# Sixteen transposes of a token pair in one burst; four PSUM banks for transposes and four for accumulators

## The chip, the cores and the metric

The kernel runs on one core of a Trainium2 chip. The metric is the time of one execution on the device in microseconds (us); of several runs the median is given. Beside the plain runs there is one profiled execution, from which the trace comes.

## The reference

One layer over 4096 prompt rows and 32 sample rows of width 1024, in float32:

```
h = RMSNorm(x) * norm_g
u, v, z_a, xb, z_b = split(h @ w_in)              # w_in is 1024 x 5120, five parts of 1024
v_n = LayerNorm(v)
a = u * (W_spatial v_n + b_spatial) * silu(z_a)   # per head and per chunk of 128 rows, masked
b = scale * group_linear(trailing_mean(xb) - xb) * silu(z_b)   # windows 2, 4, 8, 16
x = x + concat(a, b) @ w_out
y = RMSNorm(x) * final_g
```

Outputs are y for both groups of rows, the last rows of xb, and the normalised v rows of the sample group. The change lies where h and v are made for the prompt rows.

## The kernel before, in words

All large products are made by a scheme of seven products of 2 x 2 blocks (instead of eight), and each float32 operand is split into a high part that is rounded to the format of TensorE's fast pass (a cast on ScalarE, L479 for the rows, L119 for weights) and a low part, the rest (a subtraction on VectorE, L81). One product of the seven, numbered q = 0 to 6, is four steps along the contraction times three terms (high by high, high by low, low by high): twelve matmuls of 128 x 128 by 512 columns on L193.

The first stage (L211 to L613) takes about the first 398 us. It opens with the preparation of weights: the rows of w_in for xb times the pooling weights ("comb", transposes on L402 and products on L261), the rows of the past (L384), and the seven weight operands `wv` of v. Then it goes through sixteen pairs of row blocks, blocks 1, 2, 3, 0 of 1024 rows and four pairs in each. A pair is two tiles of 128 rows, 512 rows apart, called z = 0 and 1. For each pair:

- `load` brings the two tiles `xt` from DRAM on SP's queue (L466). There are four buffers for them, so two pairs' worth.
- `norms` takes the sum of squares on ScalarE (L294), the inverse root on VectorE (L86 to L91) and scales `xt` in place on VectorE (L307). The same call finishes LayerNorm of the v of an earlier pair: statistics on VectorE (L300, L301, L310), scaling on ScalarE (L312), and then two stores to `v_all` that ScalarE's queue issues (L538).
- `quarter(z, kh)` turns half a tile: four transposes of 128 x 128 on TensorE (L473) into one PSUM bank `tr`.
- `operands` returns seven steps. They make the seven left operands from the four quarters: x11, x12 and x22 directly from the bank, x21 by a copy on ScalarE (L502), and four sums on VectorE (L507, L508, L509, L516). Each operand is then split into an `op` tile and stored for later stages on SP's queue (L485, or L488 for the last block).
- `product(q)` runs the twelve matmuls into an accumulator bank `acc`, and `Combine.after(q)` puts the result together in the two tiles `vt` of v. For q 0, 2 and 4 ScalarE copies the bank (L167, L172, L174), otherwise VectorE adds it (L165, called from L169 on). Products 0, 2 and 4 share one bank, 3 and 6 another, 1 and 5 have one each: four banks for a pair. Product 6 adds on top of what product 3 left, after VectorE has read that.

While the products of pair n run, the steps of pair n + 1 are issued, one ahead of each product. So in the program's text each product has at most one quarter ahead of it. The first pair's operands are made in the opening. The last two pairs run interleaved (`lagged`), since there is no later pair to prepare: eight accumulators are then asked for, from the same pool. The text's order is not the order on the engines: a scheduler of the framework sets that, and also which buffer of a pool a tile gets, by its own costs. A tile that asks a full pool for a buffer waits for the last reader of the one it is given.

PSUM has eight banks of 128 x 512 float32. In the first stage three are in `ps_tr` (tag "tr") and five in `ps_acc` (tag "acc").

Of the kernel before, what the change touches and what calls it, by code (L numbers as in the profile page):

```python
# [36 lines left out]
def stream_step(ctx: ExitStack, tc, x_prompt, x_sample, state_pool, norm_g, w_in, ln_v_g, ln_v_b,  # L37
# [167 lines left out]
    def pool(name, bufs, stack=ctx, **kw):  # L205
        return stack.enter_context(tc.tile_pool(name=name, bufs=bufs, reuse_waits="tile", **kw))
# [4 lines left out]
    with ExitStack() as ph:  # L211
# [2 lines left out]
        e_p = ph.enter_context(tc.tile_pool(name="e_p", bufs=1))  # L214
        h_p = ph.enter_context(tc.tile_pool(name="h_p", bufs=6))
        op_p = ph.enter_context(tc.tile_pool(name="op_p", bufs=9))
        ps_tr = ph.enter_context(tc.tile_pool(name="ps_tr", bufs=3, space=bass.MemoryType.PSUM))
        ps_acc = ph.enter_context(tc.tile_pool(name="ps_acc", bufs=5, space=bass.MemoryType.PSUM))

        def xtile(dt=F32):  # L220
            return xt_p.tile([P, D], dt, tag="xt", name="xt")
# [1 line left out]
        def vtile():  # L223
            return v_p.tile([P, D], F32, tag="vt", name="vt")
# [4 lines left out]
        def half(dt=F32):  # L229
            return h_p.tile([P, HALF], dt, tag="h", name="h")  # L230
# [4 lines left out]
        def tr_tile():  # L235
            return ps_tr.tile([P, 512], F32, tag="tr", name="tr")
# [7 lines left out]
        def load_rows(i):  # L244
            rows_t[i] = vtile()
            nc.sync.dma_start(rows_t[i], w_in[0, i * P:(i + 1) * P, 3 * D:4 * D])
# [21 lines left out]
        def load_v_weights(c):  # L268
            v_raws[c] = a, b = [t.rearrange("p (k e) -> p k e", e=P)
                                for t in (op(F32), op(F32))]  # L270
            c0 = D + c * P
            nc.sync.dma_start(a, w_in_v[:, :, c0:c0 + P])
            nc.sync.dma_start(b, w_in_v[:, :, c0 + 512:c0 + 512 + P])
# [113 lines left out]
        pairs = []  # L387
# [69 lines left out]
        class Pair:  # L457
# [11 lines left out]
            def quarter(self, z, kh):  # L469
                tr = tr_tile()  # L470
                for kk in range(4):
                    k = 4 * kh + kk
                    nc.tensor.transpose(tr[:, kk * P:(kk + 1) * P], self.x[z][:, k * P:(k + 1) * P], ident)  # L473
                return tr
# [12 lines left out]
                    dst = xops_l[q, :, :, self.j * P:(self.j + 1) * P]  # L487
                    nc.sync.dma_start(dst, t.rearrange("p h (k t) -> p (h k) t", t=P).bitcast(F32))  # L488

            def operands(self):  # L490

                self.ops, k = {}, {}
                tt = nc.vector.tensor_tensor

                def one():
                    k["x11"] = self.quarter(0, 0)
                    self.split(0, k["x11"])

                def two():
                    x21 = self.quarter(1, 0)  # L500
                    k["x21"] = half()
                    nc.scalar.copy(k["x21"], x21)  # L502

                def three():
                    k["x22"] = self.quarter(1, 1)
                    k["s1"], k["s2"] = half(), half()
                    tt(k["s1"], k["x22"], k["x21"], ALU.add)  # L507
                    tt(k["s2"], k["s1"], k["x11"], ALU.subtract)  # L508
                    tt(k["x21"], k["x11"], k["x21"], ALU.subtract)  # L509

                    self.split(2, k["s2"])

                def four():
                    x12 = self.quarter(0, 1)
                    self.split(1, x12)
                    tt(k["s2"], x12, k["s2"], ALU.subtract)  # L516

                def five():
                    self.split(6, k["x22"])
                    self.split(3, k["x21"])  # L520

                return [one, two, three, four, five, lambda: self.split(4, k["s1"]), lambda: self.split(5, k["s2"])]

            def start(self):
                self.v = [vtile(), vtile()]
                va, vb = self.v
                self.c = Combine(512, acc_tile, lambda y: None, lambda: va[:, :512], lambda: va[:, 512:],
                                 lambda: vb[:, :512], lambda: vb[:, 512:])

            def product(self, q):  # L530
# [7 lines left out]
                    queue.dma_start(dst, v.rearrange("p (h c) -> p h c", c=P))  # L538

        pairs += [Pair(b, j) for b in (1, 2, 3, 0) for j in range(4)]  # L540
        first_steps = pairs[0].operands()
        before = {0: [lambda: load_rows(3), lambda: load_v_weights(1)],
                  1: [lambda: load_rows(4)],
                  2: [lambda: load_rows(5), lambda: load_v_weights(2), past.load],
# [42 lines left out]
        pa, pb = pairs[-2:]  # L587
# [12 lines left out]
            nc.scalar.copy(dst[:, :, pb.j], pb.ops[q])  # L600

        steps = pb.operands()
        pa.start()
        pb.start()
        for n, (pair, q) in enumerate(lagged(pa, pb)):
            for step in {0: steps[:2], 1: steps[2:3], 2: steps[3:4], 4: steps[4:5], 6: steps[5:6], 7: steps[6:]}.get(n, []):
# [12 lines left out]
    ps_acc = pool("ps_acc2", 6, space=bass.MemoryType.PSUM)  # L619
# [244 lines left out]
    with ExitStack() as ph:  # L864
# [220 lines left out]
        pairs = [[OutPair(z, i) for i in range(SEQ // (2 * P))] for z in range(2)]  # L1085
# [100 lines left out]
    with ExitStack() as ph:  # L1186
# [56 lines left out]
        for n in range(n_sets, len(groups)):  # L1243
# [6 lines left out]
            for m, (s, q) in enumerate(order):  # L1250
# [4 lines left out]
                k = n - n_sets - 4  # L1255
# [48 lines left out]
```

## Time and profile before

| what | value |
|---|---|
| median of three runs | 2349.31 us (2347.84 to 2350.99) |
| span of the profiled execution | 2345.9 us |
| median less that span | 3.4 us |
| TensorE (PE) busy | 2328.8 us, 99% of the span |
| VectorE (DVE) busy | 1790.2 us, 76% |
| ScalarE (ACT) busy | 896.4 us, 38% |
| GpSimd (POOL) busy | 215.1 us, 9% |
| granted TensorE clock | at 9 tenths or more in all 40 slices |
| matmuls of the first stage, L193 with `op` | 1344, that is 16 pairs of 84 |

How to read it: an engine's busy time is the sum of its instructions' time, in which TensorE's matmuls overlap each other and are therefore counted with modelled ends. A row of the timeline that ends in "x12" is a run of twelve like instructions, with its start and its length. A row of waits names what waited, an arrow, what released it, and then the total in us, the number of times, and the longest.

### The profile page before, as it was taken

Reading aid. Unit: us, or ns where it says so; the run is one execution under the profiler, and the core shown is the slowest. Engines: PE = TensorE matmul, PEld = TensorE weight load, DVE = VectorE, ACT = ScalarE, POOL = GpSimd, SP = SyncE. Lnnn points to the kernel's source line nnn. Section 1 sums busy time; section 2 is a strip of 40 time slices with the busy share of each in tenths; the row PEclk is TensorE's granted clock in tenths of the full one; section 3 lists DMA queues with packets and bytes.
Section 4 is the critical chain, followed back from the end, with each engine's and each line's share of the span. In section 5 each row is a group of like instructions: output and inputs, shape, how many; then the busy total and the mean of one; then the engine's idle time right before and its main releaser. Section 6 shows DMA issues by size and latency. Waiting matters only on the chain.

```text
span 2345.9 us, 32604 instructions
## 1 busy us (share of the span) xinstructions
PE 2328.8 (99%) x11936; PEld 1981.3 (84%) x11936; DVE 1790.2 (76%) x3318; ACT 896.4 (38%) x1603; POOL 215.1 (9%) x398
## 2 busy tenths in 40 slices
PE   8999999999999999999999999999999999999998
PEld 7878888888888888888888899999987878888877
DVE  7877786866787767877668876668777778688887
ACT  6545544433433333433334333334322333233333
POOL 1010000100021000111000110102200000000000
PEclk9999999999999999999999999999999999999999
DMA  8879977432448334483334472335587776955542
GB/s 309 316 241 279 275 255 245 142 104 89 149 144 296 99 100 134 135 300 122 108 108 148 177 262 87 101 100 164 223 294 265 252 257 232 360 171 169 159 137 90
DMA packets 325145, 445.69 MB, mean 190 GB/s; under 512 B 19324, under 2 KB 248444, under 8 KB 322296
## 3 DMA queue, kind: packets, MB, share of 16 engines
q1 hardware_dynamic: 273384, 355.05, 45.9%
q0 software_dynamic: 22288, 73.48, 8.3%
q10 hardware_dynamic: 29312, 15.08, 2.4%
q8 instruction: 94, 1.54, 0.3%
q14 instruction: 67, 0.55, 0.1%
HBM read 273.88 MB, written 169.66 MB: 189 GB/s over the span
## 4 chain that ended last, share of the span: by engine, by line
PE 95%; DMA 2%; DVE 2%; issue 0%; ACT 0%; SPq 0%; ACTq 0%; DVEq 0%
PE acc L193 66%; PE acc L712 8%; PE acc L713 8%; PE acc L714 8%; PE sp L998 2%; PE tr L473 1%; DMA wops<-raw 1%; DMA vt<-in_w_in_dram 1%; PE acc L261 0%; DMA op<-in_w_in_dram 0%; PE more L844 0%; PE more L843 0%; DVE wop L81 0%; DVE y L724 0%; PE acc L202 0%
## 5 line engine op out<-in xcount | busy, mean ns | idle before, releaser
L193 PE MATMUL acc<-slot,wop 128*128 128x512 f32 (+1 forms) x6720 | 1260.9, 348 | 1.0 <-DVE wop L81 1.0
L193 PEld LDWEIGHTS acc<-slot,wop 128*128 128x128 f32 x6720 | 1081.1, 188 | 156.5 <-DVE wop L81 1.4
L81 DVE TENSOR_TENSOR wop<-raw,wop 128x512 fp32r<-128x512 f32 (+1 forms) x510 | 353.4, 695 | 133.0 <-ACT wop L119 121.7
L119 ACT CAST wop<-raw 128x512 fp32r<-128x512 f32 x340 | 210.5, 622 | 384.4 <-PE acc L193 266.9
L712 PE MATMUL acc<-slot,wop 128*128 128x512 f32 x892 | 347.2, 389 | 1.5 <-DVE y L724 1.5
L713 PE MATMUL acc<-slot,wop 128*128 128x512 f32 x892 | 347.1, 389 | 0.0
L714 PE MATMUL acc<-slot,wop 128*128 128x512 f32 x892 | 347.0, 389 | 0.0
L193 PE MATMUL acc<-slot,op 128*128 128x512 f32 x1344 | 323.8, 395 | 0.3 <-ACT vt L167 0.2
L193 PEld LDWEIGHTS acc<-slot,op 128*128 128x128 f32 x1344 | 247.6, 188 | 51.9 <-ACT vt L167 0.7
L165 DVE TENSOR_TENSOR t<-acc,t 128x512 f32<-128x512 f32 (+1 forms) x320 | 186.7, 584 | 120.0 <-ACT t L174 65.5
L724 DVE TENSOR_TENSOR y<-acc,y 128x512 f32<-128x512 f32 x235 | 159.3, 687 | 72.6 <-PE acc L714 72.2
L712 PEld LDWEIGHTS acc<-slot,wop 128*128 128x128 f32 x892 | 167.4, 188 | 37.8 <-ACT wop L677 2.3
L714 PEld LDWEIGHTS acc<-slot,wop 128*128 128x128 f32 x892 | 167.4, 188 | 34.8
L713 PEld LDWEIGHTS acc<-slot,wop 128*128 128x128 f32 x892 | 167.4, 188 | 34.7
L677 ACT CAST wop<-raw 128x512 fp32r<-128x512 f32 x160 | 98.7, 622 | 175.2 <-PE acc L714 164.9
L81 DVE TENSOR_TENSOR wop<-sum,wop 128x512 fp32r<-128x512 f32 x200 | 136.9, 685 | 25.7 <-ACT wop L119 24.9
L1017 POOL DMA_DIRECT2D abT<-t x128 | 69.2, 541 | 843.2 <-DVE t L1029 622.7
L119 ACT CAST wop<-sum 128x512 fp32r<-128x512 f32 x136 | 84.5, 622 | 96.9 <-PE acc L193 72.0
L1040 DVE TENSOR_TENSOR t<-t 128x527 f32<-128x527 f32 (+3 forms) x160 | 111.1, 698 | 0.6
L677 ACT CAST wop<-sum 128x512 fp32r<-128x512 f32 x64 | 39.7, 622 | 119.5 <-PE acc L714 96.3
L174 ACT COPY t<-acc 128x512 f32<-128x512 f32 (+1 forms) x80 | 40.2, 504 | 107.1 <-PE acc L193 105.4
L115 DVE TENSOR_TENSOR sum<-raw 128x512 f32<-128x512 f32 x68 | 46.8, 688 | 44.7 <-DMA raw<-in_w_in_dram 44.1
(236 smaller groups left out, 1955.0 us busy)
## 6 DMA issues: line engine op xcount, KB each, us to landing
raw<-in_w_in_dram SPq DMA_DIRECT2D x102, 512.0 KB, 4.3
xops<-op SPq DMA_DIRECT2D x72, 512.0 KB, 6.1
abT<-t POOLq DMA_DIRECT2D x128, 256.0 KB, 3.8
raw<-abT SPq DMA_DIRECT2D x64, 512.0 KB, 5.0
slot<-xops SPq DMA_DIRECT2D x30, 1024.0 KB, 9.6
slot<-wops SPq DMA_DIRECT2D x14, 2048.0 KB, 9.7
xt<-in_x_prompt_dram SPq DMA_DIRECT2D x32, 512.0 KB, 5.0
raw<-v_all SPq DMA_DIRECT2D x32, 512.0 KB, 3.3
```

The source lines that it names most:

```text
L81: return nc.vector.tensor_tensor(out, src, hi.bitcast(F32), ALU.subtract)
L119: pair = nc.scalar.copy(hi, src), lo_part(lo, src, hi)
L165: add = lambda o, x, y: nc.vector.tensor_tensor(o, x, y, ALU.add)
L193: mm(acc, stationary(s, k), moving(m, k), start=fresh and n == 0, stop=n == len(terms) - 1, skip_group_check=True)
L677: nc.scalar.copy(t[:, 0], src)
L712: mm(acc, x[:, 0, k, :], w[:, k, 0, c], start=fresh and k == 0, stop=False, skip_group_check=True)
L713: mm(acc, x[:, 0, k, :], w[:, k, 1, c], start=False, stop=False, skip_group_check=True)
L714: mm(acc, x[:, 1, k, :], w[:, k, 0, c], start=False, stop=k == 3, skip_group_check=True)
L724: nc.vector.tensor_tensor(y, self.acc[bank], y, ALU.add)
L998: mm(sp[:, a, :], self.v[:, 4 * hf + a, :], WT[:, h, :], start=True, stop=True)
L1017: nc.gpsimd.dma_start(abT[row, :, t0:t0 + HALF], t[:, :HALF])
L1040: tt(nxt[:, lo:HALO + m], s[:, lo:HALO + m], s[:, lo - step:HALO + m - step], ALU.add)
```

## The change

Two edits in the first stage.

First, `operands` takes an argument, `burst`, that is true by default. Then the first step that asks for a quarter makes all four quarters of the pair, in the order (0,0), (1,0), (1,1), (0,1), and the later steps use what it made. So sixteen transposes stand together in the text, ahead of product 0 of the pair before, and fill four `tr` banks. The first pair, whose operands are made in the opening, keeps its quarters apart (`operands(False)`).

Second, `ps_tr` has four banks and `ps_acc` four. The two last pairs need up to six accumulators; `start` takes an argument for where banks come from, and the pair `pa` gets its first two from `ps_acc` and the next two from `ps_tr`.

```diff
-        ps_tr = ph.enter_context(tc.tile_pool(name="ps_tr", bufs=3, space=bass.MemoryType.PSUM))
-        ps_acc = ph.enter_context(tc.tile_pool(name="ps_acc", bufs=5, space=bass.MemoryType.PSUM))
+        ps_tr = ph.enter_context(tc.tile_pool(name="ps_tr", bufs=4, space=bass.MemoryType.PSUM))
+        ps_acc = ph.enter_context(tc.tile_pool(name="ps_acc", bufs=4, space=bass.MemoryType.PSUM))
...
-            def operands(self):
+            def operands(self, burst=True):
 
-                self.ops, k = {}, {}
+                self.ops, k, turned = {}, {}, {}
                 tt = nc.vector.tensor_tensor
 
+                def quarter(z, kh):
+                    if burst and not turned:
+                        for c in ((0, 0), (1, 0), (1, 1), (0, 1)):
+                            turned[c] = self.quarter(*c)
+                    return turned[z, kh] if burst else self.quarter(z, kh)
+
                 def one():
-                    k["x11"] = self.quarter(0, 0)
+                    k["x11"] = quarter(0, 0)
                     self.split(0, k["x11"])
...
-            def start(self):
+            def start(self, tiles=None):
                 self.v = [vtile(), vtile()]
                 va, vb = self.v
-                self.c = Combine(512, acc_tile, lambda y: None, lambda: va[:, :512], lambda: va[:, 512:],
+                self.c = Combine(512, tiles or acc_tile, lambda y: None, lambda: va[:, :512], lambda: va[:, 512:],
...
-        first_steps = pairs[0].operands()
+        first_steps = pairs[0].operands(False)
...
         steps = pb.operands()
-        pa.start()
+        banks = [tr_tile, tr_tile, acc_tile, acc_tile]
+        pa.start(lambda: banks.pop()())
         pb.start()
```

The three other calls of `self.quarter` in the steps become `quarter` in the same way. Lines behind the edit carry numbers that are six or seven higher in the changed kernel (L502 is L508, L538 is L544).

What the scheduler makes of it on TensorE, in one pair of the steady part. Before (`op` and `xt` with their numbers are single tiles; slot_132 to slot_138 hold the weights of q 0 to 6, so the slot tells which product a row is):

```order
L473 MATMUL tr_2294<-ident_75,xt_2024 128x128 x4
L193 MATMUL acc_2303<-slot_132,op_2105 128x512 x12
L473 MATMUL tr_2354<-ident_75,xt_2026 128x128 x4
L193 MATMUL acc_2361<-slot_133,op_2213 128x512 x12
L473 MATMUL tr_2375<-ident_75,xt_2026 128x128 x4
L193 MATMUL acc_2303<-slot_134,op_2191 128x512 x12
L473 MATMUL tr_2402<-ident_75,xt_2024 128x128 x4
L193 MATMUL acc_2416<-slot_135,op_2239 128x512 x12
L193 MATMUL acc_2455<-slot_137,op_2275 128x512 x3
L193 MATMUL acc_2303<-slot_136,op_2257 128x512 x12
L193 MATMUL acc_2455<-slot_137,op_2275 128x512 x9
L193 MATMUL acc_2416<-slot_138,op_2235 128x512 x12
```

The same pair on TensorE in the changed kernel (acc_2222 is the bank of products 3 and 6 of the pair before):

```order
L473 MATMUL tr_2294<-ident_75,xt_2024 128x128 x4
L473 MATMUL tr_2299<-ident_75,xt_2026 128x128 x4
L473 MATMUL tr_2304<-ident_75,xt_2026 128x128 x4
L473 MATMUL tr_2309<-ident_75,xt_2024 128x128 x4
L193 MATMUL acc_2318<-slot_132,op_2120 128x512 x8
L193 MATMUL acc_2222<-slot_138,op_2041 128x512 x12
L193 MATMUL acc_2318<-slot_132,op_2120 128x512 x4
L193 MATMUL acc_2371<-slot_133,op_2213 128x512 x12
L193 MATMUL acc_2318<-slot_134,op_2196 128x512 x12
L193 MATMUL acc_2416<-slot_135,op_2239 128x512 x12
L193 MATMUL acc_2318<-slot_136,op_2257 128x512 x12
L193 MATMUL acc_2455<-slot_137,op_2275 128x512 x12
```

The four runs of four transposes became one run of sixteen, and product 6 of the pair before now stands inside product 0 of the next.

On ScalarE before, around the same place (L294 with xt_2218 and xt_2220 is the sum of squares of the rows loaded last; L167 is the copy that product 2 waits for):

```order
L294 ACTIVATE junk_2319,ss_2318<-xt_2218 128x1024
L174 COPY vt_2098<-acc_2109 128x512
L479 CAST op_2275<-h_2187 128x512
L294 ACTIVATE junk_2321,ss_2318<-xt_2220 128x1024
L479 CAST op_2299<-tr_2294 128x512
L167 COPY vt_2292<-acc_2303 128x512
L502 COPY h_2359<-tr_2354 128x512
L312 ACTIVATE vt_2098<-vt_2098,nb_2348,rs_y_2333 128x1024
L312 ACTIVATE vt_2099<-vt_2099,nb_2348,rs_y_2333 128x1024
L538 DMA v_all_72<-vt_2098 128x8x128
L538 DMA v_all_72<-vt_2099 128x8x128
```

On ScalarE in the changed kernel:

```order
L312 ACTIVATE vt_1904<-vt_1904,nb_2169,rs_y_2154 128x1024
L312 ACTIVATE vt_1905<-vt_1905,nb_2169,rs_y_2154 128x1024
L544 DMA v_all_72<-vt_1904 128x8x128
L544 DMA v_all_72<-vt_1905 128x8x128
L174 COPY vt_2098<-acc_2124 128x512
L479 CAST op_2275<-h_2192 128x512
L479 CAST op_2314<-tr_2294 128x512
L508 COPY h_2369<-tr_2299 128x512
L294 ACTIVATE junk_2528,ss_2527<-xt_2412 128x1024
L294 ACTIVATE junk_2530,ss_2527<-xt_2414 128x1024
L167 COPY vt_2292<-acc_2318 128x512
```

The scaling of v (L312) and its two stores moved from behind L167 to ahead of L174, and the two L294, which stood apart on either side of L174, stand together right ahead of L167. They read xt_2412 and xt_2414, the rows of a pair later than those that stood there before.

More of the change, by code (lines that the diff above doesn't have):

```diff
@@ L488, in split @@
                     nc.sync.dma_start(dst, t.rearrange("p h (k t) -> p (h k) t", t=P).bitcast(F32))
-            def operands(self):
-                self.ops, k = {}, {}
+            def operands(self, burst=True):
+                self.ops, k, turned = {}, {}, {}
                 tt = nc.vector.tensor_tensor
+                def quarter(z, kh):
[3 more added lines that the diff above has]
+                    return turned[z, kh] if burst else self.quarter(z, kh)
                 def one():
-                    k["x11"] = self.quarter(0, 0)
+                    k["x11"] = quarter(0, 0)
                     self.split(0, k["x11"])
                 def two():
-                    x21 = self.quarter(1, 0)
+                    x21 = quarter(1, 0)
                     k["x21"] = half()
@@ L504, in three @@
                 def three():
-                    k["x22"] = self.quarter(1, 1)
+                    k["x22"] = quarter(1, 1)
                     k["s1"], k["s2"] = half(), half()
@@ L513, in four @@
                 def four():
-                    x12 = self.quarter(0, 1)
+                    x12 = quarter(0, 1)
                     self.split(1, x12)
```

## The prediction

> **What bounds the kernel now.** I read the page first: busy shares and the chain that ended last.
>
> ```profile
> PE 2328.8 (99%) x11936; PEld 1981.3 (84%) x11936; DVE 1790.2 (76%) x3318; ACT 896.4 (38%) x1603; POOL 215.1 (9%) x398
> PE 95%; DMA 2%; DVE 2%; issue 0%; ACT 0%; SPq 0%; ACTq 0%; DVEq 0%
> ```
>
> TensorE is busy for 99% of the span and carries 95% of the chain. A change pays only by what it takes off TensorE's queue or off one of its few waits, and costs by what it makes TensorE wait for. So the next view is the list of waits of TensorE alone, over the whole program.
>
> ```profile
> PE tr L402 <- DMA vt<-in_w_in_dram: 1.9, 1, 1.9
> PE acc L712 <- DVE y L724: 1.5, 2, 1.1
> PE tr L402 <- ACT h L406: 1.4, 2, 1.0
> ...
> PE acc L193 <- DVE wop L81: 1.0, 1, 1.0
> PE tr L473 <- ACT ppast L384: 0.7, 1, 0.7
> ...
> PE acc L193 <- ACT vt L167: 0.2, 1, 0.2
> ```
>
> Each row is total us, times, longest. None is a wait inside the steady part of the first stage. The windows of one token pair each say the same: TensorE 21.00 of 21, with VectorE at 80% and the DMA engines full.
>
> ```profile
> core 0: us, PE busy (x) PEld busy (x) DVE busy (x) ACT busy (x) POOL busy (x), PEclk, DMA share, GB/s
> 231.00:252.00 21.00, 21.00 (x101) 17.32 (x100) 16.80 (x37) 10.46 (x17) 0.00 (x0) 1.00 1.06 281
> 294.00:315.00 21.00, 21.00 (x101) 17.34 (x100) 16.79 (x37) 10.47 (x17) 0.00 (x0) 1.00 0.98 312
> ```
>
> Then TensorE in order of time, through one pair (columns: start, us, engine, line).
>
> ```profile
> 230.99 0.60 PE L473 MATMUL tr<-ident,xt 128*128 128x128 f32 x4
> 231.34 3.02 PE L193 MATMUL acc<-slot,op 128*128 128x512 f32 x12
> 234.20 0.60 PE L473 MATMUL tr<-ident,xt 128*128 128x128 f32 x4
> ...
> 240.99 11.18 PE L193 MATMUL acc<-slot,op 128*128 128x512 f32 x48
> 252.00 0.49 PE L473 MATMUL tr<-ident,xt 128*128 128x128 f32 x3
> ```
>
> A pair takes 252.00 − 230.99 = 21.01 us. Durations hold the pipeline's latency; only differences of starts count.
>
> **What a run of transposes costs.** The end of the stage has a run of eight beside runs of four, and then 144 products without a transpose.
>
> ```profile
> 357.12 1.03 PE L473 MATMUL tr<-ident,xt 128*128 128x128 f32 x8
> 357.91 2.98 PE L193 MATMUL acc<-slot,op 128*128 128x512 f32 x12
> 360.73 0.60 PE L473 MATMUL tr<-ident,xt 128*128 128x128 f32 x4
> 361.08 3.02 PE L193 MATMUL acc<-slot,op 128*128 128x512 f32 x12
> 363.94 0.60 PE L473 MATMUL tr<-ident,xt 128*128 128x128 f32 x4
> 364.30 32.95 PE L193 MATMUL acc<-slot,op 128*128 128x512 f32 x144
> 397.08 1.30 PE L193 MATMUL acc<-slot,wop 128*128 128x512 f32 x5
> ```
>
> One product matmul is (397.08 − 364.30)/144 = 0.2276 us, so twelve are 2.73. Eight transposes and twelve products took 360.73 − 357.12 = 3.61, four and twelve 363.94 − 360.73 = 3.21. So a run of four costs 0.48, a run of eight 0.88, and two runs joined save 2 × 0.48 − 0.88 = 0.08. That is the switch from transposes to products. The nearest other row is the spacing inside a run in the opening:
>
> ```profile
> 1.36 3.25 PE L251 MATMUL tr<-ident 128*128 128x128 f32 x14 [1.36 <-POOL ident masks.py:199]
> 4.69 1.10 PE L402 MATMUL tr<-ident,vt 128*128 128x128 f32 x8
> ...
> 12.69 1.04 PE L402 MATMUL tr<-ident,vt 128*128 128x128 f32 x8
> 13.56 3.62 PE L261 MATMUL acc<-op,h 128*128 128x256 f32 x16
> ```
>
> There eight take 13.56 − 12.69 = 0.87, 0.109 each. Twelve more at 0.109 on top of 0.48 make a burst of sixteen 1.79, against 4 × 0.48 = 1.92: 0.13 per pair, 0.04 per run that is gone.
>
> The order of TensorE's instructions has 62 runs of L473 before and 20 now (twelve of sixteen; the others are the first pair, which keeps its quarters, and bursts that the scheduler cut). 42 fewer, at 0.04 to 0.08: 1.8 to 3.4 us less. I take 3.4: the row of eight is from the same stage and has both ends of the run in it. The number of transposes and products is the same, so nothing else leaves TensorE.
>
> **What the change adds: waits.** Three engines feed the burst and the products around it. Durations for the walk are from the grouped rows of the steady windows (the number after "|" is the total, then mean ns of one):
>
> ```profile
> L165 DVE TENSOR_TENSOR vt<-acc,vt 128x512 f32<-128x512 f32 x16 | 11.0, 690 | 11.8 <-ACT vt L174 8.9 <-PE acc L193 2.4
> L307 DVE SCALAR_TENSOR_TENSOR xt<-xt,rs_y,g_bc 128x1024 f32<-128x1024 f32 x8 | 9.9, 1282 | 0.1
> L90 DVE SCALAR_TENSOR_TENSOR rs_t<-rs_t,na 128x4 f32<-128x4 f32 x12 | 1.9, 162 | 0.4
> L312 ACT ACTIVATE vt<-vt,nb,rs_y 128x1024 f32<-128x1024 f32 x8 | 9.5, 1237 | 11.4 <-DVE nb L310 11.4
> L294 ACT ACTIVATE junk<-xt 128x1024 bf16<-128x1024 f32 x8 | 8.5, 1057 | 0.0
> L294 ACT ACTIVATION_READ_ACCUMULATOR junk<-xt 128x1 f32 x8 | 1.5, 189 | 0.0
> L174 ACT COPY vt<-acc 128x512 f32<-128x512 f32 x4 | 2.3, 587 | 6.9 <-PE acc L193 6.9
> 363.80 0.37 ACTq L538 DMA_DIRECT2D v_all<-vt  x1
> ```
>
> First, the burst needs both halves of x normalized (L307 twice), where a run of four needed one. VectorE's row of work that ends there starts with the L165 that reads the last product of the pair before. From it to the second L307 the new order has twelve instructions of 512 columns, fifteen small ones and the two L307: 12 × 0.69 + 15 × 0.2 + 2 × 1.28 = 13.9 us (0.2 is 0.162 and its handover). TensorE reaches the burst after nine products of q 0 and five whole products: 69 × 0.2276 = 15.7. So 1.8 us are spare, and I cost it at nothing; the cover is those five products.
>
> Second, product q 6 of a pair adds into a bank that L165 (y22) must have read, and that L165 follows L174. L174 now stands in ScalarE's queue behind the two L312 and the two DMA issues: 13.9 + 0.2 + 2 × 1.24 + 2 × 0.4 + 0.59 = 18.0, and L165 ends at 18.7. The scheduler has put q 6 behind the burst and some products of the next pair, at 15.7 + 1.79 + 8 × 0.2276 = 19.3. Spare 0.6, with every duration at its full length, though they overlap by a tenth. Nothing again. Four accumulator banks are just the four that one pair holds; a new pair's bank is one that the pair before gave back five products earlier, except the first, given back by L174, above.
>
> Third, the loads. With four xt buffers, the load of a pair waits for the burst two pairs before to have read its buffer, as it waited for the last quarter. But ScalarE's queue has moved: in three steady pairs both L294 on the newly loaded rows stand ahead of L167, which q 2 waits for. Before, an L294 came most of a period after its load. The first load can go 12 × 0.109 = 1.3 after the burst starts, the second at 1.8. q 2 is due at 1.79 + 36 × 0.2276 = 10.0 (products q 0, the late q 6, q 1). Ahead of it stand the second L294 (1.06 + 0.19) and L167 (0.59, as L174), so the second load has to land by 8.1, 6.3 after its issue. What loads took, in the steady part and then in the whole run:
>
> ```profile
> DMA to landing us min/median/max: 3.6/4.8/7.0
> DMA to landing us min/median/max: 3.6/5.0/10.5
> ```
>
> At the median nothing is lost; at 7.0 it is 0.7 × 3 = 2.1 us, at 10.5 it is 12.6. Since the DMA share is about 1 and two loads now go out 0.5 us apart behind stores, I take 0.8, a little over a third of the 2.1.
>
> SP's queue holds the same stores and loads in another order; a load that stands behind a store waits for VectorE's half of that operand, which is made earlier in the period than the burst. The first pair and the opening keep their order on ScalarE; the last two pairs hold their two late accumulators in transposing banks, freed by copies that stand before L167 in the queues. I cost all of this at nothing, within 1 us either way.
>
> **The sum.** −3.4 + 0.8 = −2.6 us. The profiled execution has a span of 2345.9; the median of the runs is 2349.3, so 3.4 us lie outside the span and are not touched. 2349.3 − 2.6 = 2346.7. About 0.2%, 4.7 us, is what a measurement of this kernel tells from no change: this gain lies inside.
>
> **Rivals.** (1) *The loads take it back.* The mechanism is the third above: ScalarE stands at an L294 whose rows have not landed, L167 behind it, q 2 behind that. For: the DMA share of 1.06, and 10.5 us seen once. Against: 7.0 at most in the steady part. A mild form, landing 7.3 on average in three pairs, gives 3 us back: 2349.5, the same. It decides for slower when stalls pass 3.4 + 4.7 = 8.1 us, 2.7 in each of the three, landing at 9.0; near 10.5 it is −3.4 + 12.6 = +9.2: 2358.5. (2) *More is gained.* The fourth transposing bank also ends waits of the opening, 1.4 (L406) and 0.7 (L384), and the earlier last burst the wait of 1.0 at the next stage's first operand: −3.4 − 3.1 = −6.5, 2342.8. For: those rows. Against: the opening has loads at full DMA speed, and TensorE would mostly wait for the next thing. (3) *The clock falls.* [...] The fourteen opening transposes took 3.25/14 = 0.23 each, those after them 0.109: half speed. If every sixteen-burst brought 3.25 us of half speed, 1.6 us more each, twelve would cost 19.5: 2365.4. Against it: the opening itself, where nothing but transposes ran, and the next transposes were at full speed. [...] The opening rows disagree with that, since they warmed on transposes alone; so it gets 2 in 100.
>
> **How the numbers follow.** The forecast as summed, between −4.7 and −0.5: 0.66. Rival 1 mild, within 0.2%: 0.10; rival 1 in full, slower: 0.10. Rival 2: 0.12. Rival 3: 0.02. So faster 0.12, same 0.76, slower 0.12. The range: −3.4 and 2 us of the unpriced on the low side, 2343.5; on the high side rival 1 up to where it nearly decides, 2352.5. Left out are rival 3, rival 1 in full and half of rival 2: 0.18.
>
> **What would show it.** Right: runs of sixteen L473 that take near 1.7 to 1.8 us to the next product; a steady pair of 20.8 to 20.9 us instead of 21.01; TensorE's list of waits with no row of the first stage above 1 us; the second stage starting 2 to 4 us earlier. Wrong: rows of TensorE waiting for L167, L165 or L307 in the first stage; ScalarE waiting at L294 for xt; a granted clock under 1.00 after bursts; or pairs of 21.0 us in spite of bursts, which would say that the switch costs nothing. Loads that land over 8 us after issue in the three pairs would be rival 1.

## The result, and the profile after

| | before | changed |
|---|---|---|
| median of seven runs | 2347.84 us (2346.82 to 2350.99) | 2354.95 us (2352.07 to 2358.06) |
| span of the profiled execution | 2345.9 us | 2356.1 us |

The ratio is 1.0031, with a 95% interval of 1.0022 to 1.0041: the change makes the kernel slower by 0.3%, 7.1 us. The profiled execution of the changed kernel is the slowest of its seven (2358.06 us), 10.2 us over the profiled execution before in span. The readings below explain that execution's 10.2 us; the medians differ by 7.1.

The page's busy shares, which stood at 99%, 84%, 76%, 38% and 9% before:

```profile
PE 2331.0 (99%) x11936; PEld 1986.3 (84%) x11936; DVE 1779.5 (76%) x3318; ACT 898.9 (38%) x1603; POOL 219.6 (9%) x398
```

The shares tell nothing: the loss is 0.4% of the span. The list of TensorE's waits (what waited, what released it, total us, times, longest) does:

```profile
PE acc L193 <- ACT vt L167: 4.7, 4, 2.2
PE acc L719 <- DVE y L731: 3.3, 2, 1.8
PE acc L193 <- ACT vt L172: 2.2, 1, 2.2
...
PE acc L193 <- ACT op L479: 1.1, 1, 1.1
```

The first and third rows are new: products wait for ScalarE to copy an accumulator bank, 6.7 us in four pairs (the fifth wait, 0.17, is in the opening and stood there before). TensorE's timeline shows a pair with such a wait and two pairs without:

```profile
234.55 1.91 PE L473 MATMUL tr<-ident,xt 128*128 128x128 f32 x16
236.21 8.42 PE L193 MATMUL acc<-slot,op 128*128 128x512 f32 x36
246.47 15.47 PE L193 MATMUL acc<-slot,op 128*128 128x512 f32 x60 [1.84 <-ACT vt L167]
261.79 1.91 PE L473 MATMUL tr<-ident,xt 128*128 128x128 f32 x16
...
321.56 1.91 PE L473 MATMUL tr<-ident,xt 128*128 128x128 f32 x16
323.22 19.30 PE L193 MATMUL acc<-slot,op 128*128 128x512 f32 x84
342.37 1.91 PE L473 MATMUL tr<-ident,xt 128*128 128x128 f32 x16
...
405.73 3.79 PE L193 MATMUL acc<-slot,wop 128*128 128x512 f32 x16
```

Undisturbed, a burst takes 323.22 − 321.56 = 1.66 us to the next product and a pair 342.37 − 321.56 = 20.81 (21.01 before). But the 60 products behind the wait took 261.79 − 246.47 = 15.32 us, where 60 × 0.2276 is 13.66. The windows of 6 us behind each of the four waits say why (columns: window, TensorE's busy time, instructions, granted clock, DMA share, GB/s):

```profile
147.18:153.18 6.00, 6.00 (x19) 0.72 0.54 215
205.76:211.76 6.00, 6.00 (x19) 0.72 0.31 113
223.52:229.52 6.00, 6.00 (x26) 1.00 0.75 198
246.47:252.47 6.00, 6.00 (x19) 0.72 0.73 192
```

Behind waits of 2.16, 2.20 and 1.84 us the granted clock was 0.72 over 6 us, which is 3.36 us at half: 1.68 us lost each time. Behind the wait of 0.53 it was 1.00. The seven runs differ in this: their mean granted clock is 0.997 in the slowest, the profiled one, 0.998 in two of the others, and 0.999 in the rest, among them the three fastest.

Why ScalarE was late there, from its own timeline in the same pair:

```profile
236.55 0.60 ACT L508 COPY h<-tr 128x512 f32<-128x512 f32 x1
242.65 1.06 ACT L294 ACTIVATE junk<-xt 128x1024 bf16<-128x1024 f32 x1 [5.50 <-DMA xt<-in_x_prompt_dram]
...
244.80 1.06 ACT L294 ACTIVATE junk<-xt 128x1024 bf16<-128x1024 f32 x1 [1.00 <-DMA xt<-in_x_prompt_dram]
...
245.85 0.57 ACT L167 COPY vt<-acc 128x512 f32<-128x512 f32 x1
```

ScalarE stood still for 5.50 and 1.00 us at the two sums of squares, until the rows had landed; L167, which TensorE needed, stood behind them. The two loads there, on SP's queue:

```profile
L466 SPq DMA_DIRECT2D xt<-in_x_prompt_dram x2: 341/834/1327, 236.0 to 236.5; - x2
DMA to landing us min/median/max: 6.6/7.4/8.2
```

They went out 0.5 us apart, as soon as the burst had freed both buffers, and landed 6.6 and 8.2 us later. Over the whole run, ScalarE waited for L294's rows for 58.1 us against 7.0 before.

The account to the first product of the next stage (405.73, against 397.08 before, 8.65 later): waits 6.7, half clock 3 × 1.68 = 5.0, twelve bursts at 21.01 − 20.81 = 0.20 each −2.4, the opening (the second pair's long run of transposes begins at 62.20 against 63.00) −0.8. That makes 8.5. The rest of the 10.2 lies behind the stage: TensorE's wait for a sum on VectorE (L731) was 3.3 us here and 1.5 before.

### The profile page after: what moved, and what is told of

It is laid out like the page before. It is cut to its first block, busy times and chain, and to the rows that moved or that the text cites. A ratio compares the mean times of both kernels' runs of the same rounds, so it can differ in the third digit from the quotient of the medians.

```text
span 2356.1 us, 32587 instructions
## 1 busy us (share of the span) xinstructions
PE 2331.0 (99%) x11936; PEld 1986.3 (84%) x11936; DVE 1779.5 (76%) x3318; ACT 898.9 (38%) x1603; POOL 219.6 (9%) x398
## 4 chain that ended last, share of the span: by engine, by line
PE 86%; issue 9%; DMA 3%; DVE 2%; POOL 1%; ACT 0%; SPq 0%; POOLq 0%; ACTq 0%; DVEq 0%
PE acc L193 64%; PE acc L720 6%; PE acc L719 6%; PE acc L721 6%; PE sp L1005 2%; PE tr L473 1%; DMA xt<-in_x_prompt_dram 1%; DMA vt<-in_w_in_dram 1%; DMA xops<-op 1%; DMA wops<-raw 1%; POOL part L742 0%; DMA op<-in_w_in_dram 0%; PE acc L261 0%; PE tr L193 0%; DMA part<-y 0%
## 5 line engine op out<-in xcount | busy, mean ns | idle before, releaser
L193 PE MATMUL acc<-slot,op 128*128 128x512 f32 x1308 | 308.6, 395 | 8.0 <-ACT vt L167 4.7
L165 DVE TENSOR_TENSOR t<-acc,t 128x512 f32<-128x512 f32 (+1 forms) x320 | 186.7, 584 | 122.3 <-ACT t L174 66.7
L731 DVE TENSOR_TENSOR y<-acc,y 128x512 f32<-128x512 f32 x235 | 159.2, 686 | 72.3 <-PE acc L721 71.5
L174 ACT COPY t<-acc 128x512 f32<-128x512 f32 (+1 forms) x80 | 40.3, 504 | 108.6 <-PE acc L193 107.9
L165 DVE TENSOR_TENSOR vt<-acc,vt 128x512 f32<-128x512 f32 x61 | 42.0, 688 | 49.9 <-ACT vt L174 26.0
```

What stands on the lines that cost most here:

```text
L165: add = lambda o, x, y: nc.vector.tensor_tensor(o, x, y, ALU.add)
L193: mm(acc, stationary(s, k), moving(m, k), start=fresh and n == 0, stop=n == len(terms) - 1, skip_group_check=True)
L731: nc.vector.tensor_tensor(y, self.acc[bank], y, ALU.add)
```

## Experiments

The theory: ScalarE stands at an L294 whose rows have not landed, with a copy behind it that TensorE waits for, and a long wait brings a low clock on top (load theory). The rivals: four accumulator banks are too few (bank theory), and the bursts themselves bring the low clock (burst theory).

**Pinning the sum of squares.** The change, with L294 held at its place in the program.

```diff
-                    nc.scalar.activation(junk[:rows], xt[:rows], AF.Square, accum_out=ss[:, i:i + 1])
+                    sq = nc.scalar.activation(junk[:rows], xt[:rows], AF.Square, accum_out=ss[:, i:i + 1])
+                    if vs_:
+                        tc.keep_in_program_order(sq)
```

> The change with one thing added: each sum of squares (L294) of a pair's rows is pinned at its place in the program, so on ScalarE it stands behind the copy L167 of its own loop, a period later; bursts, banks and loads stay. Load theory (ScalarE stands at an L294 whose rows have not landed, L167 or L172 behind it, a product of TensorE behind that, and a low clock after each long wait): no wait of TensorE for L167 or L172 in the first stage, no slice under full clock there, pairs of 20.80 us, and about 12 x 0.21 = 2.5 us less than before: 2345.4, between 2344 and 2346.5. Bank theory (four accumulators are too few, so products wait for L167 to read a bank): the waits stay, about 2354. Burst theory (bursts of transposes cool the clock): low clock stays, about 2352.

Measured: 2345.49 us, ratio to before 0.9991 (0.9983 to 1.0000). The last of TensorE's waits, the only one for a copy of a bank, and from its timeline two pairs and the start of the next stage (lines behind the edit are two higher in this kernel):

```profile
...
PE acc L193 <- ACT vt L167: 0.2, 1, 0.2
```

```profile
62.58 1.47 PE L475 MATMUL tr<-ident,xt 128*128 128x128 f32 x12
...
270.35 1.91 PE L475 MATMUL tr<-ident,xt 128*128 128x128 f32 x16
...
311.96 1.91 PE L475 MATMUL tr<-ident,xt 128*128 128x128 f32 x16
...
393.41 3.79 PE L193 MATMUL acc<-slot,wop 128*128 128x512 f32 x16
```

```profile
60.00:398.00 338.00, 337.20 (x1613) 1.00 0.85 269
```

No product waits for L167 or L172 in the pairs, the clock is 1.00 from 60 us to the end of the stage in spite of thirteen bursts of sixteen, and two pairs take 311.96 − 270.35 = 41.61, 20.81 each. The loads are as late as in the change:

```profile
  ACT junk L294: 1.5, 1
...
DMA to landing us min/median/max: 4.0/6.1/10.1
```

Median 6.1 us to landing (6.4 in the change, 5.0 before), but ScalarE waits for them for 1.5 us instead of 58.1. So it is not the banks and not the bursts; pinning L294 removes the loss. (The scheduler set other copies anew with it, L174 ahead of L312 among them, so the pin is not the only row that moved.) The stretch from the second pair's long run of transposes to the next stage is 393.41 − 62.58 = 330.83 us, against 397.08 − 63.00 = 334.08 before: 3.25 less.

A second set of rounds of the same kernel:

> The change with each sum of squares pinned at its place, the same kernel as before, for a second set of rounds: by the load theory 12 x 0.21 = 2.5 us under the kernel before, a ratio of 0.9989; the first set gave 0.9991.

Measured: 2345.41 us, ratio 0.9990 (0.9981 to 0.9999). This version lies below both kernels, by 1.9 to 2.3 us in the medians against before; the first interval reaches up to 1.0000, so that gain is about as little as this measurement tells from nothing.

**The banks alone.** `operands(self, burst=False)`, so four and four banks without bursts.

> The change without its bursts: four banks for transposes and four for accumulators, every pair's quarters apart as before. Load theory: the order on ScalarE is that of before, so the time is that of before, 2347.8, within 1 us; a wait of the opening for a transposing bank may go, 0.7 at most. Bank theory: waits for L167 as in the change, 2353 or more. Burst theory: as before.

Measured: 2348.72 us, ratio 1.0004 (0.9995 to 1.0013). In its first stage nothing waits for L167 but the row that stood there before:

```profile
...
PE acc L193 <- ACT vt L167: 0.2, 1, 0.2
```

Against the bank theory. In the opening the wait of 0.7 for L384 went and a wait of 1.1 for L479 came. The second pair's long run of transposes begins 0.7 us earlier than before (62.33 against 63.00), but the wait for rows of w_in is 0.9 shorter in this execution (1.0 against 1.9), so no gain of the fourth bank is shown there.

**The loads of columns.** The change, with `columns()` called behind the pairs instead of at n == 6. In the change they stood between the two loads of one pair on SP's queue:

```profile
189.54 0.33 SPq L466 DMA_DIRECT2D xt<-in_x_prompt_dram  x1
...
190.88 1.25 SPq L452 DMA_DIRECT2D lvg<-in_ln_v_g_dram  x1
...
193.89 2.56 SPq L454 DMA_DIRECT2D psc<-in_pool_scale_dram  x1
...
197.17 0.38 SPq L466 DMA_DIRECT2D xt<-in_x_prompt_dram  x1
```

> The change with the three loads of columns (L452 to L454), which stood on SP's queue between the two loads of one pair, moved to the end of the first stage's pairs. Load theory: the second load of that pair goes out about 5.5 us earlier, the wait of 2.2 for L172 and the 1.7 of half clock behind it go, the three waits for L167 stay: about 2351. If the columns do not matter, because the load would have landed late anyway: 2355 with the wait for L172 still there.

Measured: 2350.66 us, ratio 1.0012 (1.0003 to 1.0022), 4.3 us under the change. TensorE's rows with a wait:

```profile
147.44 15.53 PE L193 MATMUL acc<-slot,op 128*128 128x512 f32 x60 [1.99 <-ACT vt L167]
219.56 11.20 PE L193 MATMUL acc<-slot,op 128*128 128x512 f32 x48 [0.36 <-ACT vt L167]
242.01 13.90 PE L193 MATMUL acc<-slot,op 128*128 128x512 f32 x60 [1.33 <-ACT vt L167]
```

The wait for L172 is gone, the three for L167 stay, a little shorter. Behind 1.99 the 60 products are slow (a granted clock of 0.72 over 6 us), behind 1.33 they are not (1.00).

**Early squares without bursts.** The kernel before, with both L294 of the rows loaded last brought ahead of L174 in seven pairs.

```diff
                 if q == 3 and n + 3 < len(pairs):
                     pairs[n + 3].load()
+                    if 2 <= n <= 8:
+                        squares(pairs[n + 3])
```

> The kernel before, without bursts and with five accumulators, but with the sums of squares (L294) of the rows loaded last brought forward in seven pairs: both stand ahead of the copy L174, as in the change both stood ahead of L167. Load theory: TensorE can be made to wait without any burst. The second load of a pair lands 15.4 to 17.3 us after the pair's start; with 1.25 for L294, 0.57 for a cast, 0.59 for L174 and 0.69 for L165, product 6 can go at 18.5 to 20.4, and it is due at about 18: waits of 0.5 to 2.4 in each of the seven, 3 to 10 us in all, with 1.7 more where a wait passes 1.8; 2351 to 2360. If the burst itself is needed for the loss: the time of before, 2347.8.

Measured: 2347.9 us, ratio 1.0004 (0.9994 to 1.0014). The expectation fell. ScalarE in one such pair from its timeline:

```profile
242.53 0.58 ACT L172 COPY vt<-acc 128x512 f32<-128x512 f32 x1
...
243.48 1.07 ACT L291 ACTIVATE junk<-xt 128x1024 bf16<-128x1024 f32 x1
...
245.00 1.08 ACT L291 ACTIVATE junk<-xt 128x1024 bf16<-128x1024 f32 x1
...
248.36 0.59 ACT L174 COPY vt<-acc 128x512 f32<-128x512 f32 x1 [1.69 <-PE acc L193]
```

(`squares` makes the two activations and pins them; L291 is its line.) In this pair the squares did not wait, and L174 waited for TensorE. Over the seven pairs three of the fourteen squares waited for their rows, 4.6 us in all, and TensorE waited in none. The transposes that let the loads go stand 3.2 us apart here, as in the kernel before, and the loads land sooner than I had reckoned:

```profile
DMA to landing us min/median/max: 3.5/4.1/5.9
```

Over the same stretch the change had 4.2/6.4/8.2 and the kernel before 3.6/4.5/7.0. So an L294 that stands ahead of a needed copy is not enough. In the change it stood right behind the burst that lets the load go, ahead of a copy due 10 us after the burst's start, and both loads went out together. That the spacing makes them slow is only read from these rows; no run changed the spacing alone.

**The price of a wait.** Needless copies of a bank ahead of L167 in the kernel before, without bursts (here 5, 7, 9 and 12):

```diff
             if q == 0:
-                nc.scalar.copy(self.y11(), acc[0])
+                for _ in range(self.stall):
+                    tc.keep_in_program_order(nc.scalar.copy(self.spare, acc[0]))
+                own = nc.scalar.copy(self.y11(), acc[0])
+                if self.stall:
+                    tc.keep_in_program_order(own)
```

> The kernel before, without bursts and with five accumulators, with 5, 7, 9 and 12 needless copies of the bank on ScalarE ahead of L167 in four pairs (beyond what L167 needs), so that product 2 waits. Load theory with the clock as a price of any long wait: waits of TensorE of about 1 to 5 us, and after those of some 1.8 us or more about 3.3 us at half of the granted clock, which costs 1.7 us each; after waits of about 1 us or less none. Burst theory: the granted clock stays at 1.00 through all of them, since no run of transposes is longer than before.

Inconclusive: the scheduler put other products into the waits, and TensorE's longest for a copy was 0.3 us; 2348.61 us in one run. So the same with TensorE's products and transposes pinned in the program's order:

> The kernel before, without bursts, with 5 to 17 needless copies of the bank ahead of L167 in thirteen pairs, one more in each than in the one before, and TensorE's products and transposes pinned in the program's order there, so that no other product can fill the wait. A copy takes about 0.5 us; the first is ready when product 0 ends, and product 2 comes 3.2 us later. So (k + 1) x 0.5 + 0.6 for the copy L508's counterpart that stands among them, less 3.2: waits from about 0.4 to 6.4 us in steps of 0.5. Clock as a price of any long wait: full clock behind waits up to about 1.3, and from about 1.8 on some 3.3 us at half of the granted clock, 1.7 us lost, no more behind longer waits. Burst theory (only a burst brings the low clock): full clock throughout. If the clock goes by windows of time that are not tied to the wait, the same length of wait will show both.

One run, 2428.88 us. Waits of 0.39 to 8.1 us; these are the windows behind 2.19, 5.05 and 3.81 (columns as above, granted clock after the count of instructions):

```profile
151.69:157.69 6.00, 6.00 (x28) 1.00 0.54 195
185.35:191.35 6.00, 6.00 (x17) 0.51 0.01 3
213.13:219.13 6.00, 6.00 (x17) 0.55 0.22 89
```

Waits bring the low clock without any burst: all nine of 3.81 us or more did, the four of 2.19 or less did not. The burst theory's strong form falls. So does a fixed limit at 1.8, since 1.91 and 2.19 brought none here where 1.84 had been enough in the change. So two more, with waits near 2 us in thirteen pairs; first without bursts (copies 7 and 8 in turn):

> The kernel before, without bursts, with waits of about two microseconds made for TensorE in thirteen pairs: 7 and 8 needless copies in turn ahead of L167, products and transposes pinned as in the run with 5 to 17. Waits of 1.6 to 2.6. If a free-running measure of activity decides (phase), some of the thirteen bring half a clock for about 3.3 us and others none. If only a burst of sixteen some microseconds earlier makes a wait of 2 us bring the low clock, none of the thirteen does.

then on the change with L294 pinned (copies 5 and 6 in turn):

> The change with L294 pinned, so with bursts of sixteen and no waits of its own, and with waits of about two microseconds made for TensorE in thirteen pairs: 5 and 6 needless copies in turn ahead of L167, products pinned. Waits of 1.3 to 2.6, some 6 us behind each burst. If phase decides, a mixture as without bursts, with a like share; if the burst decides, nearly all waits of 1.8 or more bring half a clock.

One run each, 2389.31 and 2390.01 us. Without bursts, behind waits of 2.25, 1.58, 2.66 and 2.19 us:

```profile
83.36:89.36 6.00, 6.00 (x28) 1.00 0.50 180
108.32:114.32 6.00, 6.00 (x28) 1.00 0.62 218
132.98:138.98 6.00, 6.00 (x21) 0.72 0.72 173
239.15:245.15 6.00, 6.00 (x21) 0.72 0.37 115
```

With bursts, behind waits of 2.27, 2.25, 1.27 and 2.25 us:

```profile
188.03:194.03 6.00, 6.00 (x20) 0.72 0.35 125
285.34:291.34 6.00, 6.00 (x26) 1.00 0.67 166
308.76:314.76 6.00, 6.00 (x26) 1.00 0.78 206
333.44:339.44 6.00, 6.00 (x19) 0.72 0.25 101
```

Of the waits between 1.9 and 2.3 us in these three runs, four of seven brought the low clock without bursts and four of seven with them; no wait under 1.8 did, all of 2.66 or more did. So the same length shows both outcomes, and the share is the same with bursts. In these runs the pairs come about every 24 us, so their outcomes repeat and are not fourteen independent trials.

The clock's own changes in the trace say more. In the change the three stretches at half speed are these (columns as above):

```profile
147.75:151.16 3.41, 3.41 (x10) 0.50 0.41 155
205.77:209.19 3.42, 3.42 (x8) 0.50 0.07 26
246.73:250.15 3.42, 3.42 (x9) 0.50 0.45 133
```

Each lasts 3.41 us, and their starts are 58.02 and 40.96 us apart, which is 17 and 12 times 3.413. The last change of the clock, at 2352.76 behind the last product, is 2205.01 us behind the first start, 646 times 3.4133. So all changes of the clock that the trace of this execution shows lie on one beat of 3.413 us, within 0.002. The beat does not start with the wait: the half speed began 0.57, 0.01 and 0.26 us after the wait's end. Cut at this beat, each of the three waits lies whole inside one beat, with 2.16, 2.20 and 1.84 us. Another wait of 1.84 in this execution, for the sum on VectorE (L731) up to 1882.63, is cut into 0.93 and 0.91, and the clock behind it was 1.00 (1882.63 to 1888.63). So it may be that where a wait of about two microseconds falls in the beat decides, bursts or not. This is my reading of the traces afterwards and is not shown: no run set the beat, and the wait of 1.92 in the opening of the kernel before, of which about 1.88 lie inside one beat counted back from the change of its clock at 2342.89, brought no low clock.

## Why the prediction was wrong, by its steps

The time lies outside the range and on the side of rival 1.

**The burst's gain** was right: 3.4 us forecast from 42 runs at 0.08; 3.25 less between the second pair and the next stage, once nothing waits, with 42 fewer runs there too: 0.077 for each. Per whole pair it was 0.20, where three runs at 0.08 would be 0.24 and the spacing rule 0.13.

**The first two covers** held: no L307 released a wait in the steady pairs, and no L165 made product 6 wait.

**The third step, the loads, failed.** It named the right mechanism, with the right three pairs and a limit of 6.3 us to landing, and then took 0.8 us for it. What was mis-sized is the landing: a median of 4.8 was taken from loads that go out 3.2 us apart, though the step itself said that they would now go out 0.5 apart. It also mixes the two loads of a pair: in the eight pairs of the kernel before that it covers, the first took 3.6 to 4.5 us, and the second, the only one that the limit is about, 5.1 to 7.0, three of eight over 6.3. In the change the loads landed after 5.8 to 8.2 us in the three pairs, and the second was past the limit in each: 8.06, 6.91 and 8.22 us, which are 1.8, 0.6 and 1.9 over 6.3 for waits of 2.16, 0.53 and 1.84. Together 4.5 us instead of 0.8; the limit was worked out well, the landing was not.

**SP's queue "at nothing" failed** in one pair: the loads of columns held the second load back by 5.5 us, 190.88 to 196.45, and L172 became late by 2.2. The step looked at stores, and not at what else stands there. Taking the columns away took 4.3 us off, for 2.20 + 1.68 reckoned.

**The price of a wait had no term for the clock.** Three waits cost 1.68 us each on top, 5.0 in all in the profiled execution, more than the gain of the change. This price differs from execution to execution: the mean granted clock of the seven runs is 0.997 to 0.999. The one wait of that length before, 1.92 in the opening, had full clock behind it (1.00 from 10.06 to 16.06). Rival 3 looked for a low clock behind bursts, which no run shows: with L294 pinned, thirteen bursts stand in a stretch at 1.00 (60 to 398 us). The clock fell behind waits.

**Rival 1 in full** gave the outcome, slower, at 0.10, and its mechanism, but not its price. The median is 2354.95. Its 2358.5 is near the profiled 2358.06 by luck, from two errors that cancel: landing 10.5 (it was 8.2 at most) and no clock. By its own point of decision, 8.1 us of stalls, the measured waits alone (6.7) would have been no slower; the clock made them so.

**Rival 2** did not come: the wait of 0.95 at the next stage's first operand is there in every run, and the opening got a wait of 1.1 for L479. The opening did end 0.8 us earlier in the change, but its waits for w_in and L406 were 0.8 and 0.6 shorter there, and no run separates the bank's part.

**Two slips in the sums.** The low bound worked out from its own terms is 2349.3 − 3.4 − 2 = 2343.9, and not 2343.5; rival 1's mild form is 2349.3 − 3.4 + 3.0 = 2348.9, and not 2349.5. Neither changes what follows.

## What to carry to other kernels

When a change frees buffers together, price the loads by what they take when issued together (6.6 and 8.2 us for two that went out 0.5 us apart here, 3.9 and 5.4 for two that went out 3.2 apart in the kernel before), and look at what now stands between their issue and a copy that the bound engine needs: a scheduler may have put the reader of fresh rows ahead of it. A wait of TensorE of two microseconds may cost nearly twice its length: here waits of 2.16, 2.20 and 1.84 us had products at half clock behind them and cost 1.68 us each on top, while others of 2.25 had full clock behind them. A gain of 0.2 us in each of a dozen pairs is lost to one such wait or two.

## What was not expected of the hardware

- The granted clock halved behind waits as short as 1.84 us, for about 3.4 us (0.72 over 6 us), and stayed full behind others of 2.25. Behind 3.81 and 5.05 it was 0.55 and 0.51 over 6 us. In the change's execution all its changes lie on one beat of 3.413 us.
- Loads of 512 KB, most of them 3.2 us apart, landed in 4.5 us in the median in the kernel before (from 95 to 335 us), the second of a pair in up to 7.0, and in 4.1 with early squares; in the change, where seven of the last ten pairs of loads went out within 3 us of each other, in 6.4.
- Sixteen transposes and the switch behind them took 1.66 us, 0.104 each with the switch in it; the opening's spacing was 0.109.
